# Bidirectional mLSTM encoder layer: the row work for a block of four chunks, done for both directions together and spread over the block before

## The chip, the cores and the metric

The kernel runs on one core of a Trainium2 chip. The metric is device time in microseconds (us) of one execution. TensorE (PE) does the matrix products, VectorE (DVE), ScalarE (ACT) and GpSimd (POOL) the elementwise work, and SyncE (SP) issues every transfer. Each engine goes through its own instructions in their written order, and they meet at semaphores.

## The reference

One hybrid layer on 2048 tokens of width 1024. Three mixers run on one normalised input (a bidirectional mLSTM, a neighbourhood attention, a cross-attention), are merged by gates, and an MLP follows. The change touches the mLSTM alone, four heads in each of two directions:

```
b = jnp.cumsum(lf, axis=-1)
d_log = jnp.where(tril, b[..., :, None] - b[..., None, :] + ig[..., None, :], -jnp.inf)
inter = b + m_st[..., None]
m_t = jnp.maximum(inter, jnp.max(d_log, axis=-1))
s = jnp.einsum('bhtd,bhsd->bhts', q, k) * jnp.exp(d_log - m_t[..., None])
w_inter = jnp.exp(inter - m_t)
num = einsum(s, v) + w_inter[..., None] * einsum(c_st, q)
den = jnp.sum(s, axis=-1) + w_inter * einsum(n_st, q)
h = num / jnp.maximum(jnp.abs(den), jnp.exp(-m_t))[..., None]
```

`lf` (log of the forget gate) and `ig` (input gate) are one number per head and token. From them come, per token, the running sum `b`, the running maximum `m`, and the rows `a = ig - b`, `r = b - m`, `w = exp(r + m of the chunk before)` and `exp(-m)`. This is the row work: the same few operations on 4 heads x 512 tokens.

## The kernel before

The layer has three phases. In phase 2, TensorE computes merge gates (`late_gates`, `gate`), a product of 24 matmuls of 128x512 per gate. After every sixth of them the code calls `tick()`, which advances the generator `ml_stream` by one step. So mLSTM instructions are put between gate matmuls. Gate results are taken out of PSUM by ACT (L599). There are two PSUM buffers for gates (`mm`) and two for most mLSTM tiles (`mx`).

`ml_stream` waits START_2 = 20 ticks, then goes through 32 slots of four ticks, forward and backward directions in turn, each with one chunk of 128 tokens (`ml_chunk`). Up to four chunks of a direction are in flight at different stages: the decay matrix (L809 on PE, L811 on ACT, L813 on POOL), scores (L827) and their product with the decay (`pt`, L829, which together with the copy L831 on ACT frees the scores' PSUM), a transposition of the keys (L838) with the scaled keys (`kw`, L844), outputs (L862, L865) and state (L871). On POOL the scaled query `qw` (L848) of a later chunk stands in the same queue; it reads the query tile `qk` (load L796) and the row weights `wb` (load L805).

Before the first chunk of a block of four chunks, `ml_block(d, b)` issues the whole row work of one direction: two loads, two scans on DVE (L749, L753), five further tensor operations on DVE, three copies or exponentials on ACT (L759, L762, L768), a store of `w`, and four small transpositions on PE (L772) of the running maximum `r_m`. The row tiles of both directions share one buffer of 36 partitions (direction 0 in rows 0 to 3, direction 1 in rows 32 to 35).

The order on PE is the order of the code. On the other engines a scheduler sets the order ahead of time, by when it believes inputs to be there and by how early the instruction stands in the code; at run time the order is fixed.

Of the kernel before, what the change touches and what calls it, by code (L numbers as in the profile page):

```python
# [12 lines left out]
F32 = mybir.dt.float32  # L13
F32R = mybir.dt.float32r
BF16 = mybir.dt.bfloat16
AF = mybir.ActivationFunctionType
ALU = mybir.AluOpType
# [6 lines left out]
TB = 512  # L24
# [56 lines left out]
class Body:  # L81
# [10 lines left out]
    def t(self, tag, shape, bufs, dt=F32):  # L92

        self.n += 1
        return self.p_a.tile(list(shape), dt, name=f"{tag}_{self.n}", tag=tag, bufs=bufs)
# [527 lines left out]
    def ml_stream(self):  # L623


        for _ in range(START_2):
            yield
        dirs = [list(range(16)), list(range(15, -1, -1))]
        live = [[], []]
        when = {0: [(2, 0)], 1: [(1, 1), (2, 1), (3, 0)], 2: [(1, 2)], 3: [(3, 0), (1, 3), (0, 1)]}  # L630
        d = 0
        while any(dirs) or any(live[0]) or any(live[1]):
            c = dirs[d].pop(0) if dirs[d] else None
            if c is not None and c % 4 == (0, 3)[d]:
                self.ml_block(d, c // 4)
            live[d] = [None if c is None else self.ml_chunk(d, c)] + live[d][:3]
            for tick in range(4):
                for age, _ in when[tick]:
                    if age < len(live[d]) and live[d][age]:
                        next(live[d][age], None)  # L640
                yield
            if len(live[d]) == 4:
                live[d][3] = None
            d = 1 - d
# [29 lines left out]
    def ml_consts(self):  # L674
        nc, p = self.nc, self.p_a
        t = lambda name, shape, dt=F32: p.tile(shape, dt, name=name)


        self.reset = t("reset", [36, TB])
        nc.vector.memset(self.reset, 1.0)  # L680
        nc.vector.memset(self.reset.rearrange("p (c t) -> p c t", t=128)[:, :, 0:1], 0.0)

        self.bd = t("bd", [36, 4, 128])
        nc.vector.memset(self.bd, 0.0)
        for d in range(2):
            nc.gpsimd.affine_select(out=self.bd, in_=self.bd, compare_op=ALU.not_equal, fill=1.0, base=-32 * d,
                                    pattern=[[-1, 4], [0, 128]], channel_multiplier=1)


        self.at, self.rd, self.rp = {}, {}, {}  # L690
        for d in range(2):
            for i in range(2):
                at = self.at[d, i] = t(f"at{d}{i}", [100, TB], F32R)
                rd = self.rd[d, i] = t(f"rd{d}{i}", [100, 4, 128], F32R)
                rp = self.rp[d, i] = t(f"rp{d}{i}", [36, TB])
                for x in (at, rd, rp):
                    nc.gpsimd.memset(x.bitcast(F32), 0.0)
                for k in range(2):
                    nc.vector.tensor_copy(rd[32 * k:32 * k + 4], self.bd[32 * k:32 * k + 4])
                    nc.vector.tensor_scalar(at[64 + 32 * k:68 + 32 * k], self.reset[32 * k:32 * k + 4], 0.0, 1.0, ALU.mult, ALU.add)  # L700
        self.carry = t("carry", [36, 1])
        nc.vector.memset(self.carry, NEG)
        self.packs = []
        self.rows = {}
        self.state = [None, None]
        self.gml = t("gml", [128, 512])
        raw = self.ev()
        nc.sync.dma_start(raw, self.a["g_mlstm"])
        nc.vector.tensor_scalar(self.gml, raw, 0.5, None, ALU.mult)
# [24 lines left out]
        nc.vector.scalar_tensor_tensor(l, f, 0.0, l, ALU.min, ALU.subtract)  # L734
        self.store(view(self.scr["lf"]), l)

    def ml_block(self, d, b):

        nc = self.nc
        n = b if d == 0 else 3 - b  # L740
        hs = slice(32 * d, 32 * d + 4)
        if d == 0:
            self.packs.append({x: self.row("r_" + x, (36, TB + (x == "m")), bufs=1) for x in "ifbmw"})
        P = {x: y[hs] for x, y in self.packs[n].items()}
        ig, lf, bs, m, w = (P[x] for x in "ifbmw")
        nc.sync.dma_start(ig, self.scr["ig"][4 * d:4 * d + 4, b * TB:(b + 1) * TB])
        nc.sync.dma_start(lf, self.scr["lf"][4 * d:4 * d + 4, b * TB:(b + 1) * TB])
        rev = (lambda x: x[:, ::-1]) if d else (lambda x: x)
        nc.vector.tensor_tensor_scan(rev(bs), self.reset[hs], rev(lf), 0.0, ALU.mult, ALU.add)  # L749
        cm, ce = (m[:, 1:], m[:, 0:1]) if d == 0 else (m[:, :TB], m[:, TB:])  # L750
        carry = self.carry[hs]
        nc.vector.tensor_copy(ce, carry)
        nc.vector.tensor_tensor_scan(rev(cm), rev(lf), rev(ig), ce, ALU.add, ALU.max)  # L753
        nc.vector.tensor_copy(carry, m[:, TB:] if d == 0 else m[:, 0:1])
        lo = slice(32 - 32 * d, 36 - 32 * d)
        at, rp = self.at[d, n % 2], self.rp[d, n % 2]
        a, r = ig, bs
        nc.vector.tensor_tensor(a, ig, bs, ALU.subtract)
        nc.scalar.activation(at[hs], a, AF.Copy)  # L759
        nc.vector.tensor_tensor(at[lo], a, at[hs].bitcast(F32), ALU.subtract)  # L760
        nc.vector.tensor_tensor(r, bs, cm, ALU.subtract)
        nc.scalar.activation(rp[hs].bitcast(F32R), r, AF.Copy)  # L762
        nc.vector.tensor_tensor(rp[lo], r, rp[hs], ALU.subtract)
        ms = (m[:, 0:TB] if d == 0 else m[:, 1:]).rearrange("p (c t) -> p c t", t=128)
        ms = ms[:, :, 0:1] if d == 0 else ms[:, :, 127:128]
        nc.vector.tensor_tensor(w.rearrange("p (c t) -> p c t", t=128), r.rearrange("p (c t) -> p c t", t=128),
                                ms.to_broadcast([4, 4, 128]), ALU.add)
        nc.scalar.activation(w, w, AF.Exp)  # L768
        self.store(self.scr["w"][d][b], w)
        p = self.ps("mx", (128, 4, 128))  # L770
        for c in range(4):
            nc.tensor.transpose(p[:, c, 0:4], cm[:, c * 128:(c + 1) * 128], self.ident[hs, hs])  # L772
        em = self.row(f"r_em{d}", (128, 4, 4))
        nc.scalar.activation(em, p[:, :, 0:4], AF.Exp, scale=-1.0)
        self.rows[d, b] = dict(at=at, rp=rp, em=em)

    def ml_chunk(self, d, c):

# [797 lines left out]
```

## Time and profile before

| | us |
|---|---|
| median of 3 runs | 2989.27 |
| lowest and highest | 2983.28, 2989.3 |
| the profiled execution | 2988.64 |
| its span, first to last instruction | 2986.9 |
| PE busy | 2910.6 (97%) |
| DVE busy | 2070.4 (69%) |
| ACT busy | 1195.1 (40%) |
| POOL busy | 237.1 (8%) |

PE is busy nearly throughout, so time is won or lost where PE waits. The clock granted to PE is listed by stretch as a share of 2.4 GHz: 1.00 or 0.50. Phase 2 lies at about 970 to 1345 us of the span.

### The profile page before, as it was taken

How to read it: one execution, taken by the hardware profiler on the slowest of the kernel's cores; microseconds unless marked ns; L12 is line 12 of the kernel's file. 1: busy time of each engine (PE TensorE's matmuls, PEld its weight loads, DVE VectorE, ACT ScalarE, POOL GpSimd, SP SyncE). 2: the span in 40 equal slices, each digit the busy share in tenths (PEclk: the TensorE clock that was granted, in tenths of full speed). 3: DMA queues.
4: the chain of work that ended last, by engine and by line, in shares of the span. 5: the costliest groups of instructions: out<-in, count | busy, mean ns of one | idle time of the engine just before them, and what ended most of it. 6: DMA issues, size and time to landing. Idle time of an engine off the chain costs nothing.

```text
span 2986.9 us, 41900 instructions
## 1 busy us (share of the span) xinstructions
PE 2910.6 (97%) x15028; PEld 2374.8 (80%) x15028; DVE 2070.4 (69%) x3557; ACT 1195.1 (40%) x2198; POOL 237.1 (8%) x389
## 2 busy tenths in 40 slices
PE   8999999999999899999999999999999999999999
PEld 6778788878877677778888888888878888888887
DVE  6676775567654765674769888666676888885666
ACT  6454654344543333342233333543312433344331
POOL 3020210011000322330000000000000000000000
PEclk9999999999999999999999999999999999999999
DMA  8776777867799667789535444766874444466655
GB/s 276 225 253 202 231 227 240 266 217 217 240 283 307 195 199 234 240 276 315 183 110 169 155 152 155 275 191 224 268 235 128 137 155 151 154 226 225 195 182 165
DMA packets 341712, 632.97 MB, mean 212 GB/s; under 512 B 29344, under 2 KB 151008, under 8 KB 341504
## 3 DMA queue, kind: packets, MB, share of 16 engines
q1 hardware_dynamic: 341504, 630.30, 65.4%
q8 instruction: 118, 1.93, 0.3%
q14 instruction: 90, 0.74, 0.1%
HBM read 453.63 MB, written 176.55 MB: 211 GB/s over the span
## 4 chain that ended last, share of the span: by engine, by line
PE 55%; DVE 2%; DMA 2%; issue 1%; ACT 0%; POOL 0%; SPq 0%; DVEq 0%; ACTq 0%; POOLq 0%
PE mm L232 18%; PE mm L234 18%; PE mm L233 18%; PE mm L1339 0%; DVE h L900 0%; DMA og<-s_o 0%; DMA wr<-in_w_units_dram 0%; DMA hf<-s_hf 0%; DVE ev L1495 0%; ACT hf L896 0%; POOL rs L325 0%; DVE acc L1488 0%; DVE ws L177 0%; DVE h L888 0%; DMA X<-s_a 0%
## 5 line engine op out<-in xcount | busy, mean ns | idle before, releaser
L232 PE MATMUL mm<-X,ws 128*128 128x512 f32 x1152 | 448.5, 389 | 0.0
L234 PE MATMUL mm<-X,ws 128*128 128x512 f32 x1152 | 448.2, 389 | 0.0
L233 PE MATMUL mm<-X,ws 128*128 128x512 f32 x1152 | 448.1, 389 | 0.0
L232 PE MATMUL mm<-hT,ws 128*128 128x512 f32 x896 | 375.6, 419 | 12.1 <-ACT cz L654 5.5
L177 DVE TENSOR_TENSOR ws<-wr,ws 128x1024 fp32r<-128x1024 f32 (+1 forms) x212 | 263.0, 1246 | 142.8 <-ACT ws L176 137.7
L234 PE MATMUL mm<-hT,ws 128*128 128x512 f32 x896 | 353.6, 395 | 0.0
L233 PE MATMUL mm<-hT,ws 128*128 128x512 f32 x896 | 353.4, 394 | 0.0
L233 PE MATMUL mm<-X 128*128 128x512 f32 x896 | 348.8, 389 | 2.5 <-DVE X L1462 2.5
L234 PE MATMUL mm<-X 128*128 128x512 f32 x896 | 348.7, 389 | 0.5 <-DVE X L1462 0.5
L232 PE MATMUL mm<-X 128*128 128x512 f32 x896 | 348.7, 389 | 0.4 <-ACT X L1461 0.4
L1461 ACT ACTIVATE X<-X 128x1024 fp32r<-128x1024 f32 x176 | 187.0, 1063 | 319.4 <-DMA X<-s_t 124.5
L1462 DVE TENSOR_TENSOR X<-X 128x1024 fp32r<-128x1024 f32 x176 | 214.3, 1224 | 132.8 <-ACT X L1461 132.0
L176 ACT ACTIVATE ws<-wr 128x1024 fp32r<-128x1024 f32 (+1 forms) x212 | 223.5, 1059 | 164.7 <-PE mm L234 91.8
L232 PE MATMUL mm<-ws,hT 128*128 128x512 f32 (+2 forms) x704 | 260.9, 371 | 9.3 <-ACT cz L654 5.1
L234 PEld LDWEIGHTS mm<-X,ws 128*128 128x128 f32 x1152 | 216.2, 188 | 45.1
L233 PEld LDWEIGHTS mm<-X,ws 128*128 128x128 f32 x1152 | 216.2, 188 | 44.9
L232 PEld LDWEIGHTS mm<-X,ws 128*128 128x128 f32 x1152 | 216.2, 188 | 44.5
L234 PE MATMUL mm<-ws,hT 128*128 128x512 f32 (+2 forms) x704 | 249.8, 355 | 1.1 <-DVE hT L434 1.1
L233 PE MATMUL mm<-ws,hT 128*128 128x512 f32 (+2 forms) x704 | 249.0, 354 | 0.3 <-DVE ws L177 0.3
L202 ACT ACTIVATE ws<-wr 128x512 fp32r<-128x512 f32 x224 | 135.3, 630 | 219.9 <-PE mm L234 139.3
L232 PEld LDWEIGHTS mm<-hT,ws 128*128 128x128 f32 x896 | 170.2, 190 | 54.1 <-issue 9.8
L234 PEld LDWEIGHTS mm<-hT,ws 128*128 128x128 f32 x896 | 169.6, 189 | 39.0
(266 smaller groups left out, 4855.3 us busy)
## 6 DMA issues: line engine op xcount, KB each, us to landing
wr<-in_w_units_dram SPq DMA_DIRECT2D x308, 512.0 KB
s_s<-u SPq DMA_DIRECT2D x32, 1024.0 KB
X<-s_s SPq DMA_DIRECT2D x64, 512.0 KB
X<-s_t SPq DMA_DIRECT2D x64, 512.0 KB
s_g<-ev SPq DMA_DIRECT2D x96, 256.0 KB
ev<-s_g SPq DMA_DIRECT2D x96, 256.0 KB
s_a<-u SPq DMA_DIRECT2D x96, 256.0 KB
X<-s_a SPq DMA_DIRECT2D x48, 512.0 KB
```

Of the source, the lines that this page charges most:

```text
L176: nc.scalar.activation(w[:, 0], raw, AF.Copy)
L177: nc.vector.tensor_tensor(w[:, 1], raw, w[:, 0].bitcast(F32), ALU.subtract)
L202: nc.scalar.activation(hi, src, AF.Copy)
L232: mm(out, lhs[0], rhs[0], start=first, stop=False)
L233: mm(out, lhs[0], rhs[1], start=False, stop=False)
L234: mm(out, lhs[1], rhs[0], start=False, stop=last)
L1461: nc.scalar.activation(hi, src, AF.Copy)
L1462: nc.vector.tensor_tensor(lo, src, hi.bitcast(F32), ALU.subtract)
```

## The change

`ml_block` is replaced by a generator `ml_rows(n)` that does the row work for block n of both directions in one go and yields between steps. `ml_stream` makes one step per tick. The rows of block 0 begin at tick 0 of the 20 ticks that were idle; those of block n + 1 begin at slot 8n + 3, five slots before they are needed. Four ticks pass between the loads and the first scan. `a`, `r` and the exponential of `w` are done once for all 36 partitions in place of once per direction. The five row tiles are allocated once and set to 0 by POOL (L711).

```diff
     def ml_stream(self):
+        rows = self.ml_rows(0)
         for _ in range(START_2):
+            next(rows, None)
             yield
+        slot = 0
...
             c = dirs[d].pop(0) if dirs[d] else None
-            if c is not None and c % 4 == (0, 3)[d]:
-                self.ml_block(d, c // 4)
+            if slot % 8 == 3 and slot < 24:
+                rows = self.ml_rows(slot // 8 + 1)
+            slot += 1
             live[d] = [None if c is None else self.ml_chunk(d, c)] + live[d][:3]
             for tick in range(4):
                 for age, _ in when[tick]:
                     if age < len(live[d]) and live[d][age]:
                         next(live[d][age], None)
+                next(rows, None)
                 yield
...
-        self.packs = []
+        self.pack = [t("r_" + x, [36, TB + 2 * (x == "m")]) for x in "ifbmw"]
+        for x in self.pack:
+            nc.gpsimd.memset(x, 0.0)
...
+    def ml_rows(self, n):
+        nc = self.nc
+        ig, lf, bs, m, w = self.pack
+        cm, a, r = m[:, 1:TB + 1], ig, bs
+        dirs = [(d, n if d == 0 else 3 - n, slice(32 * d, 32 * d + 4), slice(32 - 32 * d, 36 - 32 * d)) for d in range(2)]
+        rev = lambda d, x: x[:, ::-1] if d else x
+        for d, b, hs, _ in dirs:
+            for x, name in ((lf, "lf"), (ig, "ig")):
+                nc.sync.dma_start(x[hs], self.scr[name][4 * d:4 * d + 4, b * TB:(b + 1) * TB])
+        for _ in range(4):
+            yield
+        for d, _, hs, _ in dirs:
+            nc.vector.tensor_tensor_scan(rev(d, bs[hs]), self.reset[hs], rev(d, lf[hs]), 0.0, ALU.mult, ALU.add)
+            yield
+        for d, _, hs, _ in dirs:
+            ce = m[hs, 0:1] if d == 0 else m[hs, TB + 1:TB + 2]
+            carry = self.carry[hs]
+            nc.vector.tensor_copy(ce, carry)
+            nc.vector.tensor_tensor_scan(rev(d, cm[hs]), rev(d, lf[hs]), rev(d, ig[hs]), ce, ALU.add, ALU.max)
+            nc.vector.tensor_copy(carry, m[hs, TB:TB + 1] if d == 0 else m[hs, 1:2])
+            yield
+        nc.vector.tensor_tensor(a, ig, bs, ALU.subtract)
+        for d, _, hs, _ in dirs:
+            nc.scalar.activation(self.at[d, n % 2][hs], a[hs], AF.Copy)
+        nc.vector.tensor_tensor(r, bs, cm, ALU.subtract)
+        yield
+        for d, _, hs, lo in dirs:
+            at = self.at[d, n % 2]
+            nc.vector.tensor_tensor(at[lo], a[hs], at[hs].bitcast(F32), ALU.subtract)
+            nc.scalar.activation(self.rp[d, n % 2][hs].bitcast(F32R), r[hs], AF.Copy)
+        yield
+        for d, _, hs, lo in dirs:
+            rp = self.rp[d, n % 2]
+            nc.vector.tensor_tensor(rp[lo], r[hs], rp[hs], ALU.subtract)
+        yield
...
+        nc.scalar.activation(w, w, AF.Exp)
+        for d, b, hs, _ in dirs:
+            self.store(self.scr["w"][d][b], w[hs])
+        for d, b, hs, _ in dirs:
+            yield
+            p = self.ps("mx", (128, 4, 128))
+            for c in range(4):
+                nc.tensor.transpose(p[:, c, 0:4], cm[hs, c * 128:(c + 1) * 128], self.ident[hs, hs])
+            em = self.row(f"r_em{d}", (128, 4, 4))
+            nc.scalar.activation(em, p[:, :, 0:4], AF.Exp, scale=-1.0)
+            self.rows[d, b] = dict(at=self.at[d, n % 2], rp=self.rp[d, n % 2], em=em)
```

Three places show how this moves instructions. The first is PE at the first transpositions of phase 2. Before, those of the forward direction stand in the sixth gate (`mm_11001`), after its first six matmuls:

```order
L232 MATMUL mm_11001<-hT,ws_10832 128x512
L233 MATMUL mm_11001<-hT,ws_10832 128x512
L234 MATMUL mm_11001<-hT,ws_10832 128x512
L232 MATMUL mm_11001<-hT,ws_10832 128x512
L233 MATMUL mm_11001<-hT,ws_10832 128x512
L234 MATMUL mm_11001<-hT,ws_10832 128x512
L772 MATMUL mx_11028<-ident,r_m_11011 128x4 x4
```

Now they stand at the same place of the fourth gate (`mm_10972`), and those of the backward direction six matmuls behind them:

```order
L234 MATMUL mm_10972<-hT,ws_10619 128x512
L794 MATMUL mx_10979<-ident,r_m 128x4 x4
L232 MATMUL mm_10972<-hT,ws_10619 128x512
L233 MATMUL mm_10972<-hT,ws_10619 128x512
L234 MATMUL mm_10972<-hT,ws_10619 128x512
L232 MATMUL mm_10972<-hT,ws_10619 128x512
L233 MATMUL mm_10972<-hT,ws_10619 128x512
L234 MATMUL mm_10972<-hT,ws_10619 128x512
L794 MATMUL mx_10992<-ident,r_m 128x4 x4
```

Both have moved up by two gates, which is 48 matmuls for the forward direction.

The second place is DVE at the first two chunks, where `pt` and `kw` are the chunks' own work, `r_` and `at_` the row work of block 1, and `ws` a split of weights. Before:

```order
L829 TENSOR_TENSOR pt_1968_11154<-mx_11156,de_1967_11145 128x2x128
L749 SCALAR_TENSOR_TENSOR r_b_11647<-reset,r_f_11646 4x512
L844 TENSOR_TENSOR kw_1972_11176<-mx_11171,de_1967_11145 128x256
L753 SCALAR_TENSOR_TENSOR r_m_11648<-r_f_11646,r_m_11648,r_i_11645 4x512
L177 TENSOR_TENSOR ws_11126<-wr_11125,ws_11126 128x8x128
L754 COPY carry<-r_m_11648 4x1
L758 TENSOR_TENSOR r_i_11645<-r_i_11645,r_b_11647 4x512
L749 SCALAR_TENSOR_TENSOR r_b_11647<-reset,r_f_11646 4x512
L761 TENSOR_TENSOR r_b_11647<-r_b_11647,r_m_11648 4x512
L760 TENSOR_TENSOR at_10783<-r_i_11645,at_10783 4x512
L829 TENSOR_TENSOR pt_1982_11220<-mx_11221,de_1981_11211 128x2x128
```

Now:

```order
L851 TENSOR_TENSOR pt_1963_11156<-mx_11158,de_1962_11147 128x2x128
L866 TENSOR_TENSOR kw_1967_11178<-mx_11173,de_1962_11147 128x256
L177 TENSOR_TENSOR ws_11128<-wr_11127,ws_11128 128x8x128
L851 TENSOR_TENSOR pt_1977_11226<-mx_11227,de_1976_11217 128x2x128
L851 TENSOR_TENSOR pt_1977_11226<-mx_11228,de_1976_11217 128x2x128
L759 SCALAR_TENSOR_TENSOR r_b<-reset,r_f 4x512
```

The row work of block 1 is gone from between these chunks: it now stands ahead of the first `pt`, right behind that of block 0. The scan in the last row belongs to block 2.

The third place is SP ahead of the load of the third chunk's `qk`. Before, the row loads of block 1 stand directly in front of it:

```order
L746 DMA r_i_11645<-s_ig 4x512
L172 DMA wr_11257<-in_w_units_dram 128x1024
L747 DMA r_f_11646<-s_lf 4x512
L746 DMA r_i_11645<-s_ig 4x512
L747 DMA r_f_11646<-s_lf 4x512
L796 DMA qk_2010_11337<-s_qk 128x4x128
```

Now:

```order
L101 DMA s_w_137<-r_w 4x512
L101 DMA s_w_142<-r_w 4x512
L172 DMA wr_11263<-in_w_units_dram 128x1024
L827 DMA wb_2055_11573<-s_w_136 64x2x128 x2
L827 DMA wb_2077_11669<-s_w_143 64x2x128 x2
L818 DMA qk_2005_11348<-s_qk 128x4x128
```

The row loads have gone ahead, and two stores of `w` and four loads of `wb` stand between the weights and the `qk` load.

## Rows read from the trace of the kernel before

**Rows 1.** Waits of PE at 960 to 1360 us: us in total, times, longest

```profile
PE mx L838 <- ACT sk L831: 7.4, 3, 5.9
PE mm L232 <- DMA hT<-s_hT: 4.0, 1, 4.0
...
PE mm L232 <- ACT ev L599: 1.8, 1, 1.8
...
PE mx L827 <- ACT de L811: 2.2, 2, 1.1
PE mx L827 <- DVE C L877: 1.5, 3, 0.9
PE mx L827 <- DVE kw L844: 1.1, 1, 1.1
```

**Rows 2.** Windows: us, busy us and counts by engine, PEclk (granted clock), DMA share, GB/s

```profile
80.00:82.00 2.00, 1.93 (x12) 1.94 (x13) 1.97 (x5) 1.24 (x3) 0.00 (x0) 0.79 1.01 395
82.00:84.00 2.00, 2.00 (x5) 0.96 (x4) 1.97 (x3) 0.00 (x0) 0.00 (x0) 0.50 0.93 250
...
1008.00:1010.00 2.00, 2.00 (x11) 1.41 (x11) 1.67 (x2) 1.95 (x4) 1.43 (x2) 1.00 0.54 172
976.00:1344.00 368.00, 346.88 (x1954) 261.95 (x1953) 246.62 (x490) 141.69 (x380) 118.79 (x157) 0.99 0.72 228
...
974.00:976.00 2.00, 2.00 (x7) 1.52 (x7) 1.97 (x3) 0.43 (x2) 2.00 (x4) 0.64 1.03 385
...
1040.00:1042.00 2.00, 2.00 (x14) 1.28 (x12) 1.71 (x5) 1.01 (x2) 0.32 (x1) 0.92 0.78 244
```

**Rows 3.** Timeline of PE: start, us, what, [idle before <- releaser]

```profile
80.07 0.39 PE L232 MATMUL mm<-ws,hT 128*128 128x272 f32 x1 [2.37 <-ACT cz L654]
...
989.99 0.39 PE L232 MATMUL mm<-hT,ws 128*128 128x512 f32 x1
...
1001.19 0.41 PE L772 MATMUL mx<-ident,r_m 4*128 4x4 f32 x4
...
1007.75 0.50 PE L232 MATMUL mm<-hT,ws 128*128 128x512 f32 x1 [1.83 <-ACT ev L599]
```

**Rows 4.** Timeline of DVE at the first two scans of block 0

```profile
992.21 1.21 DVE L749 TENSOR_TENSOR_SCAN r_b<-reset,r_f 4x512 f32<-4x512 f32 x1 [3.29 <-DMA r_f<-s_lf]
993.35 1.25 DVE L753 TENSOR_TENSOR_SCAN r_m<-r_f,r_m,r_i 4x512 f32<-4x512 f32 x1
```

**Rows 5.** Timelines of SP, POOL, DVE and PE around the second chunk

```profile
1020.46 0.38 PE L838 MATMUL mx<-ident,qk 128*128 128x128 f32 x2
...
1021.77 0.55 SPq L796 DMA_DIRECT2D qk<-s_qk  x1
...
1027.04 2.08 POOL L848 TENSOR_TENSOR qw<-qk,wb 128x256 f32<-128x256 f32 x1 [7.67 <-PE mx L827]
1029.19 1.59 POOL L806 TENSOR_TENSOR rd<-bd,rp 36x512 fp32r<-36x512 f32 x1
1030.86 1.44 POOL L813 TENSOR_SCALAR_AFFINE_SELECT de<-de 128x512 f32<-128x512 f32 x1
...
1032.86 0.68 DVE L760 TENSOR_TENSOR at<-r_i,at 4x512 fp32r<-4x512 f32 x1
1033.57 0.76 DVE L829 TENSOR_TENSOR pt<-mx,de 128x256 f32<-128x256 f32 x2
...
1034.47 0.69 PE L838 MATMUL mx<-ident,qk 128*128 128x128 f32 x2 [5.89 <-ACT sk L831]
```

**Rows 6.** Three POOL lines in phase 2: count, ns min/median/max, first and last start

```profile
L806 POOL TENSOR_TENSOR rd<-bd,rp x32: 1262/1283/2275, 1000.6 to 1286.3; 36x512 fp32r<-36x512 f32 x32
...
L813 POOL TENSOR_SCALAR_AFFINE_SELECT de<-de x32: 631/637/1558, 1018.7 to 1325.9; 128x512 f32<-128x512 f32 x32
...
L848 POOL TENSOR_TENSOR qw<-qk,wb x30: 727/744/2082, 1012.2 to 1325.1; 128x256 f32<-128x256 f32 x30
```

**Rows 7.** Timeline of DVE in a slot without row work

```profile
1083.06 0.76 DVE L829 TENSOR_TENSOR pt<-mx,de 128x256 f32<-128x256 f32 x2 [1.69 <-PE mx L827]
```

More of the change, by code (lines that the diff above doesn't have):

```diff
@@ L735, in ml_logsig @@
         self.store(view(self.scr["lf"]), l)
-    def ml_block(self, d, b):
+    def ml_rows(self, n):
         nc = self.nc
[L740 to L757, printed above, removed]
@@ L758, in ml_block @@
+        for d, _, hs, _ in dirs:
[5 more added lines that the diff above has]
+            yield
         nc.vector.tensor_tensor(a, ig, bs, ALU.subtract)
-        nc.scalar.activation(at[hs], a, AF.Copy)
@@ L760, in ml_block @@
-        nc.vector.tensor_tensor(at[lo], a, at[hs].bitcast(F32), ALU.subtract)
+        for d, _, hs, _ in dirs:
+            nc.scalar.activation(self.at[d, n % 2][hs], a[hs], AF.Copy)
         nc.vector.tensor_tensor(r, bs, cm, ALU.subtract)
[L762 to L765, printed above, removed]
@@ L766, in ml_block @@
-        nc.vector.tensor_tensor(w.rearrange("p (c t) -> p c t", t=128), r.rearrange("p (c t) -> p c t", t=128),
-                                ms.to_broadcast([4, 4, 128]), ALU.add)
-        nc.scalar.activation(w, w, AF.Exp)
[L769 to L774, printed above, removed]
@@ L775, in ml_block @@
-        self.rows[d, b] = dict(at=at, rp=rp, em=em)
+        yield
[8 more added lines that the diff above has]
+        yield
+        for d, _, hs, _ in dirs:
+            ms = (m[hs, 0:TB] if d == 0 else m[hs, 2:TB + 2]).rearrange("p (c t) -> p c t", t=128)
+            ms = ms[:, :, 0:1] if d == 0 else ms[:, :, 127:128]
+            nc.vector.tensor_tensor(w[hs].rearrange("p (c t) -> p c t", t=128), r[hs].rearrange("p (c t) -> p c t", t=128),
+                                    ms.to_broadcast([4, 4, 128]), ALU.add)
```

## The prediction

> **What bounds the kernel now.** I read the page first (PE is busy nearly throughout), then the windows of phase 2, since only there the change moves anything. From 976 to 1344 us PE is busy 346.9 of 368 us, DVE 246.6, POOL 118.8 [rows 2]. So the order of gate matmuls on PE sets the end. Work on the other engines counts only where PE waits for it, and 121 idle us on DVE can hide it otherwise. Next I read PE's waits [rows 1] and placed each in the timeline. Those near row work are the wait of 1.8 us for a gate's copy (L599), 1.1 us for `kw`, 5.9 us at the second chunk's key transposition, and, at the beginnings of blocks 2 and 3, all of the 2.2 and 1.5 us at L827 and the 7.4 - 5.9 = 1.5 us that is left of L838: 5.2 us.
>
> A long wait costs twice, because the clock falls to 0.50 behind it. After the wait of 5.89 us PE goes on at 1034.47 [rows 5] with the clock low until about 1040.3 (at 1040 to 1042 it is 0.92, so low for 0.32 us): 5.8 us at half speed, 2.9 us lost. After the wait of 4.0 us, which ended at 968.9, the clock was low until 975.4 (0.64 in 974 to 976): 6.5 us, 3.2 lost. A wait of 2.37 us at 80.07 [rows 3] was followed by 0.79 and then 0.50 in two windows, at least 0.4 + 1.0 = 1.4 us lost. After the 1.83 us at 1007.75 the clock stayed at 1.00 [rows 2, 3]. So row work costs PE today 1.8 + 1.1 + 5.9 + 2.9 + 5.2 = 16.9 us in all: no more can be won.
>
> **The change part by part.**
>
> *A, the new wait at the first transpositions.* The 20 idle ticks looked free, but PE's order is that of the code. Step 12 of `ml_rows(0)` puts the forward transpositions 48 matmuls ahead of where they stood. Before, they began at 1001.19; sixteen groups of three matmuls back, PE is at 989.99 [rows 3]. Their input does not come earlier by as much: the first scan began at 992.21, when `r_f` landed (the load of a log that is itself computed at the beginning of phase 2), and the second scan, which makes `r_m`, ended at 993.35 + 1.25 = 994.6 [rows 4]. The new order on DVE keeps these two scans first, and the load is behind the same store. So PE waits 994.6 - 990.0 = 4.6 us where it did not wait before. For the clock I take 2.9 us, between the 2.9 and 3.2 of the two waits that are nearest in length, at their lower end because the backward transpositions, six matmuls on, give DVE's other two scans time (2.5 us; six matmuls at half speed take about 2.6). **A costs 7.5 us.** Bounds: 6.0 (clock at 1.4) and 9.8 (the loads land 2 us later, since SP now issues a `qk`, a `v` and a weights load ahead of them, and the clock costs 3.2).
>
> *B, the gate's copy.* L599 stood on ACT behind a copy of block 0's backward row, which waited for DVE; PE waited 1.83 us [rows 3]. Block 0's rows begin no later than before, and PE is 7.5 us later, so ACT has time. But block 1's four copies now stand ahead of the sixth gate's copy, so a similar wait can come back there. **B gains 1.8**, bounds 0 and 1.8.
>
> *C, the first two chunks.* Before, `kw` stood behind a scan that waited for a row load: 1.1 us. Then came the 5.9. Its chain [rows 5]: `qk` of the third chunk is issued at 1021.77; POOL's `qw`, which reads it, begins at 1027.04. The row names a matmul as releaser, but `qw` reads only what two loads bring, and stands in front of the second chunk's `rd` and decay mask on POOL. These three take 2.08 + 1.59 + 1.44 = 5.11 us beside DVE's row work, and 0.74 + 1.28 + 0.64 = 2.66 us by their medians [rows 6]. The mask ends at 1032.30, and DVE is then busy with row operations (the last is L760) until `pt` at 1033.57, 1.27 us later. PE goes on 0.90 us after that. With no row work between these chunks, `pt` comes 2.45 + 1.27 = 3.7 us earlier. The `qk` load can leave up to 0.9 us earlier: its tile is free after the first chunk's key transposition, which ended at 1020.46 + 0.38 = 1020.84, and SP has the 5.7 us by which PE is now late (A less B) to clear the loads ahead of it. PE would then go on at 1034.47 - 4.6 = 1029.9 and, without the `kw` wait, arrive 1.1 us before its old 1028.6, at 1027.5. A wait of 2.4 us stays, because the cause that is left is a load and not row work. It is as long as the one at 80.07, so the clock costs about 1.4 in place of 2.9. **C gains 4.6 + 1.5, about 6.** Bounds: 1.3 (only the 1.27 us of DVE go) and 9.9 (all of 1.1 + 5.9 + 2.9).
>
> The Trainium skill's page "SBUF — State Buffer", section "Who interferes with whom", says that a DVE instruction with two SBUF inputs and a GpSimd instruction that reads SBUF exclude each other: the second one blocks until the first is done. The `qw` of 2.08 us agrees (0.74 plus the scan's 1.25 is 1.99). If POOL's stretch were long for another reason, C would gain 2.45 less, and the sum would come to little over 1 us won.
>
> *D, blocks 2 and 3.* Their rows are spread, but since `r_m` is one buffer, the second scan of a direction must wait until PE has transposed that of the block before, five slots on. So a scan and two tensor operations stand together ahead of one `pt`: 1.25 + 0.68 + 0.68 = 2.6 us (the scan as in [rows 4], the others at the length of L760 [rows 5], whose tile has as many elements a row). In a slot without row work DVE is idle 1.69 us before `pt` [rows 7]. The rest, 0.9 us a block, I count as a wait of PE. **D gains 5.2 - 1.8 = 3.4**, bounds 0 and 5.2.
>
> *The rest is hidden.* Eight tensor operations (8 x 0.68 = 5.4 us of DVE) and four exponentials go; DVE's 121 idle us make that worth nothing. Five fills of the row tiles on POOL come while its next work waits for block 0's rows. The eight groups of transpositions are the same on PE, only elsewhere.
>
> Sum: 7.5 - 1.8 - 6 - 3.4 = -3.7 us. The profiled execution took 2988.6 (its span 2986.9 and 1.7 around it), 0.6 under the median of the three runs. Forecast: **2984.9 us**. What a measurement of this kernel can tell from no change is about 0.2%, or 6 us, so this is most likely no change that can be told.
>
> **The rivals.**
>
> 1. *The wait at the second chunk goes wholly.* If `qk` lands 2.4 us earlier, PE does not wait there and the clock stays up: C is 9.9, and the time is 2988.6 + 7.5 - 1.8 - 9.9 - 3.4 = 2981.0. For it: SP's load is late today because SP is busy. Against it: four `wb` loads and a weights load now stand right ahead of that load. 0.25.
> 2. *Slower: the wait at the second chunk stays.* If the `qk` load comes as late behind the stores of `w` for block 1 and the `wb` loads, and POOL is held as before, C is 1.3: 2988.6 + 7.5 - 1.8 - 1.3 - 3.4 = 2989.6, and 2991.9 with A at 9.8. It is slower from the point at which C gains less than 2.3. For it: the two stores of `w` on SP, ahead of the load, wait for the last operation of block 1's rows. 0.20.
> 3. *The new neighbour of POOL.* Block 1's rows now stand beside the four `rd` products of POOL, so DVE and POOL hold each other there; the rows end later, ACT's copies with them, and PE waits at the eighth gate for the sixth gate's copy. At the size of the old wait (1.83), B falls to 0: 2986.7. It is the skill's rule again, by which this place would not be free; no run here shows it. 0.07.
> 4. *The new wait does not arise*, because PE reaches the fourth gate late for another reason: 2988.6 - 1.8 - 6 - 3.4 = 2977.4. Nothing in the trace of before holds PE there. 0.05.
>
> The forecast itself has the remaining 0.43.
>
> **How the numbers follow.** The forecast's own range is 2983 to 2989 (A and D by about 2 either way). To the fast side the range reaches through rival 1, to 2978 (D at 5.2 as well); to the slow side through rival 2 with A at its upper bound, to 2993. Faster by over 0.2%: rival 4, most of rival 1 and the forecast's edge, 0.32. Slower by over 0.2%: rival 2 with A high and D at 0, 0.12. Within 0.2%: 0.56.
>
> **What would show it.** A: in the new trace PE has a wait of 4 to 5 us for `r_m` at L794 near 990 us, released by DVE's L765, with the clock at 0.50 behind it. B: no wait of PE for L599 near 1000 to 1025. C: the wait at the key transposition (now L860) between 1 and 3.5 us, POOL's three operations near 2.7 us together, and `kw` without a wait. D: PE's waits in blocks 2 and 3 of about 2 us in all. I am wrong if L794 does not wait, if the wait at the second chunk is over 4 us or nil, or if waits appear after 1200 us that were not there, where only transfers and the outputs are at work.

## The result

The changed kernel takes 2993.03 us (median of 20 runs, 2987.96 to 2998.81), the kernel before 2988.41 us in the same session (20 runs, 2980.35 to 2993.09). The ratio is 1.0021, 95% interval [1.0014, 1.0029]: about 4.6 us slower, where 3.7 us faster was forecast. The median lies just above the range. (The ratios here and below are those on record; they are not quotients of the two medians, which here give 1.0015, and differ from these by up to 0.001.)

### The profile page after: what moved, and what is told of

It reads as the page before. It is cut to its first block, busy times and chain, and to the rows that moved or that the text cites. A ratio compares the mean times of both kernels' runs of the same rounds, so it can differ in the third digit from the quotient of the medians.

```text
span 2986.3 us, 41896 instructions
## 1 busy us (share of the span) xinstructions
PE 2907.5 (97%) x15028; PEld 2374.9 (80%) x15028; DVE 2066.3 (69%) x3549; ACT 1193.7 (40%) x2194; POOL 237.9 (8%) x394
## 4 chain that ended last, share of the span: by engine, by line
PE 53%; DMA 2%; DVE 2%; issue 1%; ACT 1%; POOL 0%; SPq 0%; DVEq 0%; ACTq 0%; POOLq 0%
PE mm L232 18%; PE mm L234 17%; PE mm L233 17%; DMA wr<-in_w_units_dram 1%; PE mm L1361 0%; DMA hf<-s_hf 0%; DVE h L922 0%; DVE ws L177 0%; DVE ev L1517 0%; DVE acc L1510 0%; ACT hf L918 0%; POOL rs L325 0%; DMA og<-s_o 0%; DMA X<-s_s 0%; DMA X<-s_a 0%
## 5 line engine op out<-in xcount | busy, mean ns | idle before, releaser
L232 PE MATMUL mm<-X,ws 128*128 128x512 f32 x1152 | 448.5, 389 | 0.0
L234 PE MATMUL mm<-X,ws 128*128 128x512 f32 x1152 | 448.2, 389 | 0.0
L232 PE MATMUL mm<-hT,ws 128*128 128x512 f32 x896 | 376.6, 420 | 13.5 <-ACT cz L660 5.8
L234 PE MATMUL mm<-hT,ws 128*128 128x512 f32 x896 | 354.6, 396 | 0.0
L234 PE MATMUL mm<-X 128*128 128x512 f32 x896 | 348.7, 389 | 0.5 <-DVE X L1484 0.5
L232 PE MATMUL mm<-X 128*128 128x512 f32 x896 | 348.7, 389 | 0.0
L232 PE MATMUL mm<-ws,hT 128*128 128x512 f32 (+2 forms) x704 | 260.1, 369 | 7.6 <-ACT zif L528 5.2
L234 PEld LDWEIGHTS mm<-X,ws 128*128 128x128 f32 x1152 | 216.3, 188 | 45.0
L232 PEld LDWEIGHTS mm<-X,ws 128*128 128x128 f32 x1152 | 216.3, 188 | 44.6
L234 PE MATMUL mm<-ws,hT 128*128 128x512 f32 (+2 forms) x704 | 249.7, 355 | 1.6 <-DVE hT L434 1.6
L232 PEld LDWEIGHTS mm<-hT,ws 128*128 128x128 f32 x896 | 170.3, 190 | 55.0 <-issue 8.1
L234 PEld LDWEIGHTS mm<-hT,ws 128*128 128x128 f32 x896 | 170.3, 190 | 39.3
```

The source lines that it names most:

```text
L232: mm(out, lhs[0], rhs[0], start=first, stop=False)
L234: mm(out, lhs[1], rhs[0], start=False, stop=last)
```

## The profile after

The profiled execution took 2988.03 us with a span of 2986.3 us. First PE's waits at 960 to 1360 us, as in [rows 1]:

```profile
PE mx L794 <- issue: 6.7, 1, 6.7
PE mx L893 <- DVE hm L929: 6.2, 4, 2.6
PE mx L860 <- ACT sk L853: 4.3, 4, 1.8
PE mm L232 <- ACT ev L599: 4.2, 3, 2.1
PE mm L232 <- DMA hT<-s_hT: 2.8, 1, 2.8
PE mx L849 <- DVE C L899: 1.3, 1, 1.3
PE tr L926 <- DVE h L922: 1.1, 1, 1.1
```

The new wait at the transpositions (L794) is there. The 5.9 us at the second chunk's key transposition (L838, now L860) are gone: no wait there is over 1.8. But the gates' copies (L599) now cost 4.2 us in three waits, against 1.8 in one, and `hm` (L929) stands at 6.2 us. Where the first of these lie, in the timeline of PE:

```profile
980.83 0.50 PE L232 MATMUL mm<-hT,ws 128*128 128x512 f32 x1 [2.11 <-ACT ev L599]
...
994.68 0.55 PE L794 MATMUL mx<-ident,r_m 4*128 4x4 f32 x4 [6.74 <-issue]
...
1020.49 0.50 PE L232 MATMUL mm<-hT,ws 128*128 128x512 f32 x1 [1.62 <-ACT ev L599]
...
1037.94 0.44 PE L860 MATMUL mx<-ident,qk 128*128 128x128 f32 x2 [1.72 <-ACT sk L853]
```

Windows of the same kernel, with the columns of [rows 2]. The eighth and ninth column are the granted clock and the DMA share:

```profile
976.00:1344.00 368.00, 343.74 (x1946) 261.21 (x1945) 238.35 (x479) 139.66 (x383) 116.90 (x159) 0.98 0.73 228
988.00:990.00 2.00, 0.00 (x0) 0.00 (x0) 0.00 (x0) 0.21 (x1) 0.00 (x0) 1.00 0.92 306
990.00:992.00 2.00, 0.00 (x0) 0.00 (x0) 0.00 (x0) 0.00 (x0) 0.00 (x0) 0.63 0.91 336
992.00:1000.00 8.00, 5.32 (x18) 3.99 (x19) 7.64 (x9) 0.89 (x3) 0.00 (x0) 0.50 0.54 145
1000.00:1002.00 2.00, 2.00 (x9) 1.64 (x8) 1.90 (x4) 1.93 (x4) 0.00 (x0) 0.81 0.58 229
```

The clock falls during the wait and stays at 0.50 from the restart at 994.68 to 1000, then 0.81 on average for 2 us: some 6 us at half speed, 3 us lost.

To see where time goes I measured, in PE's timeline, from one gate matmul (L232 to L234) to another: from the first of phase 2 to the 241st (ten gates, in which the first three chunks start: the fill), from there to the 637th (the middle, up to block 3's transpositions, with which the row work ends), and to the 985th (the end). The second number of a pair is a second profile of the same kernel (runs before_again and after_again below).

| us | before | after | difference of the means |
|---|---|---|---|
| fill, ten gates | 77.1, 76.4 | 81.6, 83.4 | +5.7 |
| middle | 171.5, 171.4 | 167.8, 169.3 | -2.9 |
| end | 135.7, 133.1 | 136.9, 136.2 | +2.1 |

The sum, +4.9, is about the loss that the medians show. The fill repeats well: e10 and e6 below, whose one edit is used only behind it, add 77.4 to the kernel before and 81.7 to the changed one. The end does not: the two profiles of the kernel before differ by 2.6 us there, more than the +2.1. So the question is what makes the fill 5.7 us longer although its largest old wait is gone, and what happens at the end, where no row work is left.

## The experiments

The tables below give times after the first gate matmul of phase 2, since phase 2 begins up to 8 us earlier or later from one execution to the next (phase 1 is the same code in all kernels). I started from the theory that the new wait is the loss, and from rivals.

**e1**, the transpositions of block 0 later, and **e2**, only the forward ones early, in the kernel before:

```diff
 # e1, in ml_rows of the changed kernel
+        for _ in range(0 if n else 6):
+            yield
         for d, b, hs, _ in dirs:
             yield
             p = self.ps("mx", (128, 4, 128))
 # e2, in ml_stream of the kernel before
-        for _ in range(START_2):
+        for k in range(START_2):
+            if k == 12:
+                self.ml_block(0, 0)
             yield
```

> The changed kernel, with block 0's two groups of transpositions (L794) 36 matmuls further down PE's order (12 groups of three); DVE's, ACT's and the queues' work is as it was. Theory 1: the new wait of 6.7 us at these transpositions, with about 3 us of low clock behind it, is the cause of the loss. PE then reaches them at about 996.1, after r_m (994.6), so it does not wait, the clock stays at 1.00, and the time is 9 to 10 us under that of the changed kernel, 5 us under that of the kernel before (about 2983.5, ratio to before 0.9983). Rival 1: the time at the transpositions is slack that PE must wait out anyway, since the row products and the loads behind them end when they ended; then waits of 5 us and more appear at the first decay products (L831 in the changed kernel) or at the second chunk's key transposition, and less than 3 us come back (2990 or more). Rival 2: the loss comes from the new waits after 1200 us (hm, 6.2 us in four against 3.5): then the same.

> The kernel before, with nothing but block 0's forward row work (ml_block(0, 0)) issued eight ticks earlier, so that its transpositions stand where the changed kernel has them, 48 matmuls earlier in PE's order. Theory 1: PE gets there at about 988 to 990, r_m is ready at about 994.6 at the earliest, so it waits 5 to 7 us with the clock at 0.50 behind, and as nothing is gained elsewhere the time is 7 to 10 us over that of before (2996 to 2998, ratio 1.0025 to 1.0034). Rival 1: later waits (1.8 us for the sixth gate's copy, 5.9 us at the second chunk's key transposition) shrink by what PE is late, and the time is within 3 us of before.

e1: 2991.1 us, ratio to before 1.0017 [1.0008, 1.0026]. e2: 2986.8, ratio 0.9998 [0.9989, 1.0007]. Theory 1 falls by the times, from both sides. In e1 the wait at the transpositions is gone, and the fill takes 81.2 us, as in the changed kernel: the time is lost some 20 us further on, at the eighth gate (the expectations call it the seventh). Timelines of e1, ACT, DVE, POOL and PE:

```profile
1011.49 1.28 ACT L770 ACTIVATE at<-r_i 4x512 fp32r<-4x512 f32 x2 [9.52 <-DVE r_i L768]
1012.80 0.60 ACT L599 ACTIVATE ev<-mm 128x512 f32<-128x512 f32 x1
...
1001.90 4.46 DVE L759 TENSOR_TENSOR_SCAN r_b<-reset,r_f 4x512 f32<-4x512 f32 x2
...
997.50 7.78 POOL L830 TENSOR_TENSOR rd<-bd,rp 36x512 fp32r<-36x512 f32 x4 [23.45 <-DVE rp L780]
...
1013.45 0.79 PE L232 MATMUL mm<-hT,ws 128*128 128x512 f32 x1 [6.70 <-ACT ev L599]
```

A gate's copy stands on ACT behind two copies of block 1's rows, which wait 9.5 us for DVE; and DVE does block 1's scans at 1002, right behind the rest of block 0's row work, beside POOL's four `rd` products: two scans take 4.46 us there, where one takes 1.21 in [rows 4].

e2 has one thing against it. In its profile PE waits 5.6 us at the transpositions, as was meant, and the fill takes 80.0 us against 76.4 to 77.4. POOL then waits 5.2 us for PE's first decay product, and the first key transposition comes at 57.8 us after the first gate in place of 51.5. This execution was the slowest of e2's twelve (2991.5 us). The median shows no loss, and the interval leaves room for 0.07%, about 2 us: most of the wait with its low clock is slack, but not surely all.

**after_again** and **before_again** are the two kernels unchanged.

> The changed kernel once more, for a second profile. Theory 1: again 6 to 7 us of wait at L794 near 990, 1.5 to 2 us for the copies of gates 0 and 6, and no wait over 2 us at the second chunk. Rival 2: the waits for hm after 1200 us are again about 6 us in all; if they are 3.5 or less, they differ from one execution to the next and are no part of the change.

> The kernel before once more, for a second profile. Theory 1: the waits of phase 2 as in its first profile (4 us at the start for hT, 1.8 us for the sixth gate's copy, 5.9 us at the second chunk's key transposition), to within 1 us each. Rival 2: the waits for hm after 1200 us stay at 3.5 us.

They took 2993.44 and 2987.33 us. after_again waits 5.95 us at L794, 1.8 and 1.3 us for the two gate copies, but 3.0 us at the second chunk; for `hm` 6.0 us in four waits. before_again waits 2.9 us for hT, 1.6 for the sixth gate's copy, 5.89 at the second chunk, and for `hm` only 1.3. The differences that the theory names are those of the kernels, not of one execution.

**e3 and e4**: block 1's rows held back until the second chunk's `pt`, with and without the edit of e1. **e5**: e1 with block 1's copies on DVE. **e6**: `hm`'s first copy on DVE.

```diff
 # e3, e4: in ml_stream, ml_rows and ml_chunk
-            if slot % 8 == 3 and slot < 24:
+            if slot in (4, 11, 19):
...
+        if n == 1:
+            nc.vector.tensor_tensor(self.held, lf[:, 0:1], self.pt[0:36, 0, 0:1], ALU.add)
...
-        pt = self.t(f"pt{d}", [128, 4, 128], 1)
+        pt = self.pt = self.t(f"pt{d}", [128, 4, 128], 1)
 # e5: for n == 1, so for rp too
-            nc.scalar.activation(self.at[d, n % 2][hs], a[hs], AF.Copy)
+            nc.vector.tensor_copy(self.at[d, n % 2][hs], a[hs])
 # e6: in ml_chunk
-        nc.scalar.activation(hm[:, 0], p, AF.Copy)
+        nc.vector.tensor_copy(hm[:, 0], p)
```

> The kernel of e1 (late transpositions of block 0), in which block 1's row work is also held back: its loads, and with them its scans and copies, wait for one small DVE operation that reads the second chunk's pt (about 1033 in e1), and start one slot later in the code. Theory 2: PE's time between 1000 and 1035 us hangs on ACT, where the gates' copies (L599) stand behind copies of block 1's rows (6.7 us at the seventh gate in e1) and behind DVE's scans, lengthened beside POOL's rd products. Held back, these waits go (only the 1.4 us behind block 0's r_w stays), and PE reaches the second chunk 6 to 8 us earlier than in e1; the time is 5 to 8 us under e1, 2 to 4 under the kernel before (ratio 0.9986 to 0.9993). Rival 3: the fill's other chain (block 0's w, its store, the wb loads on SP, POOL's qw in front of rd and the decay mask) ends when it ended, so the two key transpositions (4.3 us in e1) wait as much longer, and less than 2 us are won against e1. Rival 4: the held rows now collide with chunks (DVE ahead of pt, as in the kernel before), with new waits of 3 us or more between 1040 and 1090.

> The changed kernel with block 1's row work held back as in e3, its transpositions of block 0 where the change put them. Theory 2: the wait at the transpositions stays at 6 to 7 us (plus the clock), the wait for the sixth gate's copy (1.3 to 1.6) goes, and DVE's work ahead of the first chunks gets shorter, so it gains 2 to 4 us on the changed kernel (2989 to 2991). Rival 3: no gain, as the wb loads hold the second chunk.

> The kernel of e1, with the four copies of block 1's rows (at and rp) done by DVE in place of ACT; its scans stay as early as in e1. If ACT's queue alone is the cause (theory 2), the 6.7 us at the seventh gate go to under 2, and the time is 4 to 6 us under e1, whether or not the fill follows; if the fill's other chain binds (rival 3), the wait at the gate goes too but comes back at the key transpositions, and less than 2 us are won.

> The changed kernel with the first copy of hm (L928) done by DVE in place of ACT, for all second-pass chunks. Theory 3: of the loss, 2 to 3 us come from after 1200 us, where ACT now has a weight conversion that waits for its load in front of the copy of hm, and PE waits for hm (6 us in all against 1.3 to 3.5 before). With the copy on DVE those waits fall to 2 us or less, and the time is 3 to 5 us under the changed kernel (2988 to 2990). Rival: DVE is late itself there, hm's waits stay over 4 us, and the time stays within 2 us.

| | us | ratio to before | fill, us | end, us |
|---|---|---|---|---|
| e3 | 2986.07 | 1.0006 [0.9996, 1.0015] | 77.5 | 138.3 |
| e4 | 2990.05 | 1.0013 [1.0004, 1.0022] | 78.0 | 137.3 |
| e5 | 2992.31 | 1.0023 [1.0014, 1.0033] | 82.7 | 136.8 |
| e6 | 2988.69 | 1.0001 [0.9990, 1.0011] | 81.7 | 133.9 |

Holding block 1's rows shortens the fill to 77.5 and 78.0 us, with the transpositions late or early (e4 still waits 4.2 us there). In the times less came of it: e3 missed the 0.9986 to 0.9993 that theory 2 asked, and the interval of e4 overlaps that of the changed kernel. e5 gains nothing, but it does not clear ACT: the exponential of block 1's `w` stayed there, and the first chunk's `de` stands behind it. Timelines of ACT and PE in e5:

```profile
1024.82 0.63 ACT L793 ACTIVATE r_w<-r_w 36x512 f32<-36x512 f32 x1 [11.50 <-DVE r_w L791]
1025.35 0.57 ACT L841 ACTIVATE de<-mx 128x512 f32<-128x512 f32 x1
...
1025.98 1.22 PE L857 MATMUL mx<-qk 64*128 64x128 f32 x6 [9.55 <-ACT de L841]
```

The wait moved from the gate's copy to the first chunk's scores. So the fill follows block 1's rows as a whole (e3, e4); which engine's queue hands the delay on, e5 does not tell. e6 shortens the end by 2.6 us (against the mean of the two profiles after). Theory 3 also asked that the waits for `hm` fall to 2 us or less, and they did not; only the long ones went (2.6 and 3.2 us in the two profiles after). PE's waits in e6:

```profile
PE mx L893 <- DVE hm L929: 5.1, 5, 1.6
```

**e7**: block 0's rows apart, forward first, by the old `ml_block`. **e8**: that, block 1 held, and the fills moved. **e9**: e8 with e6. **e10**: the kernel before with e6, as control.

```diff
 # e7, in ml_stream (ml_block is the old one, on the new tiles)
-        rows = self.ml_rows(0)
+        rows = iter(())
...
+            if slot < 2:
+                self.ml_block(slot, 3 * slot)
             slot += 1
 # e8 adds, beside the hold of e3 (in ml_consts and ml_rows)
-        for x in self.pack:
-            nc.gpsimd.memset(x, 0.0)
...
+            for x in (ig, bs, m[:, 1:TB + 1], w):
+                nc.vector.tensor_scalar(x, self.reset, self.pt[0:36, 0, 0:1], 0.0, ALU.mult, ALU.mult)
```

> The changed kernel with block 0's row work as in the kernel before: each direction alone and the forward one first, its transpositions at their old place; blocks 1 to 3 stay joint and early, and the fills of the row tiles stay on POOL. Theory 4: what the change lost at the beginning of phase 2 is a longer chain to the first chunk, since the forward rows now wait for the backward scans (w's exponential starts 40.9 us after the first gate matmul against 31.2, at's copy 33.8 against 27.3). Done apart, w's exponential starts at 33 or less (1.6 us late from POOL's fills), and the first key transposition at 54 to 58 us after the first gate in place of 63.5. Block 1's early rows still hold ACT and DVE, so the time is 2 to 4 us under the changed kernel. Theory 2 alone (block 1's rows are the whole cause): the first key transposition stays at 61 or later, and the time is within 1.5 us of the changed kernel.

> Both: block 0's row work apart and forward first as in the kernel before, block 1's held until the second chunk's pt as in e3, and the fills of the row tiles (four, since r_f needs none) moved from POOL's beginning to DVE behind that pt. Theories 2 and 4 together: gml is ready 13.4 us after the first gate as before, the first key transposition comes at 51 to 53 us (51.3 before), the second at 59 to 62 (65.2 before, since no row work stands between these chunks), the third 6 us earlier than before; blocks 1 to 3 keep their 2.5 us. So 5 to 8 us under the kernel before (ratio 0.9973 to 0.9984), with up to 3 us lost again to the waits for hm after 1200 us. Rival 3: the wb loads hold the second chunk, its key transposition stays at 64 to 66, and the gain is 1 to 3 us (0.9990 or more).

> The kernel of e8 with hm's first copy on DVE as in e6. Theory 3: the stretch after 1200 us is 2 to 3 us shorter than in the changed kernel, whatever order ACT was given, so 1 to 4 us under e8, and 6 to 10 under the kernel before (0.9967 to 0.9980).

> The kernel before with hm's first copy on DVE alone, the control for e6 and e9. If the waits for hm after 1200 us are the changed kernel's own (theory 3), it gains at most 1.5 us (0.9995 to 1.0005); if this copy is better on DVE anyway, it gains 3 us or more, and e6's gain says nothing on the change.

e7: 2989.8 us, 1.0006 [0.9998, 1.0015]. e8: 2987.8, 1.0008 [0.9999, 1.0018]. e9: 2982.18, 0.9986 [0.9977, 0.9995] (0.9967 to 0.9980 was asked). e10: 2985.64, 1.0001 [0.9992, 1.0010]. Milestones of the fill, in us after the first gate matmul, from one profile each (in the table, `w` and `wb` are of block 0):

| begins at | before | after | e4 | e7 | e8 | e11 |
|---|---|---|---|---|---|---|
| first scan (DVE) | 23.3 | 27.1 | 26.0 | 24.3 | 23.1 | 22.8 |
| exponential of the forward `w` (ACT) | 31.4 | 41.3 | 40.3 | 32.5 | 31.3 | 31.0 |
| exponential of the backward `w` (ACT) | 39.9 | 41.3 | 40.3 | 41.1 | 39.9 | 39.6 |
| issue of the first forward `wb` load (SP) | 35.5 | 51.9 | 45.7 | 36.5 | 35.3 | 35.0 |
| issue of the first backward `wb` load (SP) | 42.4 | 55.7 | 47.1 | 48.4 | 42.4 | 42.1 |
| second `qw`, backward (POOL) | 46.7 | 59.4 | 51.5 | 53.9 | 47.4 | 46.3 |
| first chunk's mask (POOL) | 49.8 | 62.5 | 56.0 | 57.0 | 51.0 | 49.3 |
| first key transposition (PE) | 51.5 | 64.0 | 58.0 | 60.7 | 57.2 | 51.2 |
| second key transposition (PE) | 65.5 | 72.8 | 66.4 | 70.1 | 65.7 | 61.1 |
| third key transposition (PE) | 76.9 | 81.4 | 77.8 | 80.3 | 76.2 | 72.6 |

This is the chain that sets the changed kernel's fill: the rows give `w`; `w` is stored and comes back as `wb`; `qw` reads `wb`, and two of them stand on POOL in front of the first chunk's mask, the second of them the backward direction's; the mask releases `pt`, and `pt` the scores' PSUM, which PE needs. Done jointly, the forward rows wait for the backward scans, and the exponential of the forward `w` starts 9.9 us later. That of the backward `w`, which the second `qw` needs, is only 1.4 us late. The other 11 us of the second `qw` are lost on the way to its load. Timelines of DVE, SP and POOL in the changed kernel (965.1 is the first gate):

```profile
1008.51 3.54 DVE L759 TENSOR_TENSOR_SCAN r_b<-reset,r_f 4x512 f32<-4x512 f32 x2
...
1012.41 2.58 DVE L765 TENSOR_TENSOR_SCAN r_m<-r_f,r_m,r_i 4x512 f32<-4x512 f32 x2
...
1015.37 1.23 DVE L177 TENSOR_TENSOR ws<-wr,ws 128x1024 fp32r<-128x1024 f32 x1
...
1009.14 7.81 SPq L172 DMA_DIRECT2D wr<-in_w_units_dram  x2
...
1020.84 2.53 SPq L827 DMA_DIRECT2D wb<-s_w  x4
...
1024.57 1.60 POOL L870 TENSOR_TENSOR qw<-qk,wb 128x256 f32<-128x256 f32 x1 [1.79 <-DMA wb<-s_w]
1026.25 1.29 POOL L828 TENSOR_TENSOR rd<-bd,rp 36x512 fp32r<-36x512 f32 x1
1027.61 0.64 POOL L835 TENSOR_SCALAR_AFFINE_SELECT de<-de 128x512 f32<-128x512 f32 x1
```

SP stands 7.0 us at a weights load, whose tile DVE frees with a split of weights (`ws`); the split stands behind block 1's scans, and all `wb` loads behind the weights load. Ahead of the backward ones SP waits 1.5 us more, to store the gate whose copy ends the wait at 1020.49. From the second `qw` on, POOL goes to the mask without a wait. A second path meets this one at `rd`, which also waits for PE's own first decay product: 0.7 us in the kernel before (nothing in before_again), 2.5 in e4, 1.6 in e8. Where it does, PE's order is the later of the two.

e7 brings the forward `w` back, and finds block 1's rows in the way further down: the backward `wb` leaves at 48.4 and the second `qw` starts at 53.9 against 46.7. The first key transposition comes at 60.7, where theory 4 asked 54 to 58, and the fill takes 80.4 us. e8 has both and still stands at 57.2 (and at 1.0008, where 0.9973 to 0.9984 was asked); its third place is in DVE's and POOL's timelines of e8:

```profile
1020.22 0.69 DVE L917 SCALAR_TENSOR_TENSOR og<-og,gml 128x512 f32<-128x512 f32 x1 [6.21 <-DMA og<-s_o]
1020.83 0.75 DVE L893 TENSOR_TENSOR pt<-mx,de 128x256 f32<-128x256 f32 x2
...
1015.58 0.64 POOL L877 TENSOR_SCALAR_AFFINE_SELECT de<-de 128x512 f32<-128x512 f32 x1
```

The mask is done at 1016.2, but `pt` stands behind a product for `og`, a tile that only the later half of the chunks uses, which waits 6.2 us for its load. The gap that the held rows left on DVE was given to it by the scheduler. Neither rival 3 nor my numbers had that.

**e11** (on e9) and **e12** (on e8) hold `og` back too.

```diff
+        if c == (5, 10)[d]:
+            og = self.t(f"og{d}", [128, 512], 1)
+            nc.vector.tensor_copy(og[:, 0:1], pt[:, 0, 0:1])
```

> The kernel of e9 with one more hold: the tile og, whose load and product belong to the second pass, gets a one-column copy of the sixth chunk's pt first, so that the scheduler can't put its product into DVE's queue ahead of the first chunk's pt. Theory 5: in e8 and e9 the first key transposition waits 4.0 and 5.3 us (57 us after the first gate against 51.3 before) only because pt stands behind og, whose load lands at 1020.2, while the decay mask is done at 1016.2. Held, it comes at 52 to 53, the second at 60 to 62, the third at 71 to 73 (76.7 in e9), and the time is 3.5 to 5 us under e9 and 7 to 9 under the kernel before (ratio 0.9970 to 0.9977). Rival 3: the second chunk stays at 65 to 66 because of the third chunk's qk load, which POOL's qw waits for; then less than 1.5 us are won.

> The kernel of e8 (hm's copy on ACT as in the changed kernel) with the same hold of og. Theory 5: the beginning of phase 2 as in e11; after 1200 us the waits for hm as ACT's order has them, so 3.5 to 5 us under e8 and 2 to 4 over e11 (ratio to before 0.9980 to 0.9992). Rival 3: within 1.5 us of e8.

e11: 2976.07 us against 2982.32 of before in the same session, 0.9972 [0.9961, 0.9983]. e12: 2980.88, 0.9992 [0.9983, 1.0001], 4.8 us over e11 where 2 to 4 was asked. The key transpositions came within 1 us of where theory 5 put them, and rival 3 falls; the fill takes 72.8 and 72.6 us. e11 is faster than both kernels. Its waits of PE at 960 to 1360 us:

```profile
PE mx L905 <- ACT sk L895: 5.0, 5, 2.9
PE mx L938 <- DVE hm L974: 4.8, 6, 1.6
PE mm L232 <- ACT ev L599: 2.8, 3, 1.6
PE mm L232 <- DMA hT<-s_hT: 2.6, 1, 2.6
PE mx L891 <- DVE C L944: 1.4, 1, 1.4
```

**The end.** Timelines of ACT and PE in the changed kernel, near 1250 us:

```profile
1247.04 0.60 ACT L599 ACTIVATE ev<-mm 128x512 f32<-128x512 f32 x1 [2.23 <-issue]
1250.79 1.06 ACT L176 ACTIVATE ws<-wr 128x1024 fp32r<-128x1024 f32 x1 [3.14 <-DMA wr<-in_w_units_dram]
1251.75 0.58 ACT L928 ACTIVATE hm<-tr 128x512 fp32r<-128x512 f32 x1
...
1255.16 0.66 PE L893 MATMUL mx<-v,kw 128*64 128x129 f32 x8 [2.60 <-DVE hm L929]
```

ACT's timeline at the same work in before_again:

```profile
1249.65 0.60 ACT L599 ACTIVATE ev<-mm 128x512 f32<-128x512 f32 x1 [1.06 <-PE mm L234]
1250.15 0.59 ACT L906 ACTIVATE hm<-tr 128x512 fp32r<-128x512 f32 x1
...
1253.12 1.06 ACT L176 ACTIVATE ws<-wr 128x1024 fp32r<-128x1024 f32 x1 [2.38 <-DMA wr<-in_w_units_dram]
```

The scheduler changed places of `hm`'s copy and a weight conversion, which waits 3.1 us for its load. With the copy on DVE the time falls by about 0.2% from e8 to e9 and from e12 to e11, each in one session, and not at all in the kernel before (e10). From the changed kernel to e6 the ratio falls as much, but by the medians e6 is still 3.2 us over the kernel before, against 4.6. In the profiles the end is shorter by 2.4 to 2.7 us of some 5 to 6; where the rest lies stays open. That the conversion's wait in front of the copy is what the edit removes is argued from these rows, since the waits for `hm` fell so little in e6.

## Why the prediction was wrong

**Sign and premise.** The step that failed is the first one: "the order of gate matmuls on PE sets the end", so that waits of PE can be added up one by one. That holds in the middle. In the fill it does not: the chain in the table above runs beside PE, and a wait that is removed on PE is met again where this chain ends. That is why the 10 us at the transpositions did not come back when removed (e1), and cost at most about 2 us when put in alone (e2, with the reservation made there). With it failed the step "The rest is hidden": row work that was moved ahead of the first chunk had no price in the sum, and the second `qw`, which stands in front of that chunk's mask, starts 12.7 us later.

**A** was right in place and kind, and too small: 6.7 us of wait and 3 of clock, for 4.6 and 2.9. Part of it is that phase 2 began 3.8 us earlier in this execution and PE arrived at 987.9. But counted from the first gate the scan's load was also 3.8 us late (27.1 against 23.3), and my upper bound had 2. Then its cost was booked as a loss of its own, which e1 refutes, and e2 by its times.

**The fills were not hidden.** "Five fills of the row tiles on POOL come while its next work waits" is true of POOL, but they slow down DVE beside them. DVE's timeline at the last copies of the constants, in before_again:

```profile
979.83 0.41 DVE L699 CAST rd<-bd 4x512 fp32r<-4x512 f32 x1
```

The same copy in after_again, with POOL's timeline beside it:

```profile
978.20 0.73 DVE L705 CAST rd<-bd 4x512 fp32r<-4x512 f32 x1
...
977.86 0.80 POOL L711 MEMSET r_w<- 36x512 f32 x1
```

`gml` is ready 15.0 us after the first gate in place of 13.4, and so is all that follows on DVE; the first gate's copy, which stands behind it, costs the wait at 980.83. With the fills moved (e8) it is 13.4 again.

**B** had the wrong sign. The old wait went, one of 1.6 us came at the eighth gate, and block 1's four copies stand in front of the gate's copy on ACT: this is rival 3, which I gave 0.07. Its size there is small because PE comes late; in e1, where PE comes earlier, it is 6.7 us.

**C** came near its place and was still the wrong count. From the first to the second key transposition it took 14.0 us before and takes 8.8 now, 5.2 us less where about 6 was forecast (10.1 in after_again, 3.7 less than in before_again). POOL's three operations, at 1034.21 to 1037.01, take 2.65 us together, as forecast; that the scan alone held them before was read wrongly, since it ended 0.4 us after `qw` had begun and a split of weights ran beside most of it. But the row work did not vanish from there: it moved ahead of the first chunk, whose key transposition went from 51.5 to 64.0 us. I followed what left the place and not where it went, though the order on DVE showed it "right behind that of block 0", and I did not see that doing both directions together puts the forward rows, the ones needed first, behind the backward scans, nor that SP's loads would stand behind it: "SP has the 5.7 us by which PE is now late" to clear them, I wrote, and SP spent 7.0 us waiting for DVE.

**D** was right: 3.4 forecast, 2.9 measured over the middle, where PE's waits fell from 5.2 to 2.5 us.

**After 1200 us** I named new waits as what would make me wrong, and gave them no price. They cost 2.1 us in the profiles. Rival 2 ended on the right side, but not by its cause, which was a wait at the second chunk that stays: 1.7 us were left of 5.9 (3.0 in after_again).

Together: fill +5.7 (forecast 7.5 - 1.8 - 6 = -0.3), middle -2.9 (-3.4), end +2.1 (0). In the profiles the fill carries most of the error. The times leave the shares open: e6 repairs only the end, with a fill of 81.7 us, and its ratio is 1.0001, while e12 repairs only the fill and has 0.9992. That block 1's early rows hold the chain is shown by e3 and e4; that the joint rows of block 0 with the fills on POOL do, by e3 against e11 and e12 (77.5 us against 72.8 and 72.6; in none of these does the first `pt` wait behind `og`); that `og` does in their absence, by e8 against e12. The joint rows and the fills were not parted, and how much each costs alone can't be said, since they hide one another.

## What to carry to other kernels

Where a pipeline fills, look for the chain from the first load to the first steady step and follow what moves onto it: the waits of the busy engine there are largely one slack seen at several places, and removing one shows the next. Follow it through the queue that issues the loads, too: one load that waits for its buffer holds all behind it (7.0 us here). Work that is joined is as late as its latest input, so what is needed first is better done apart. And where a scheduler orders the engines ahead of time, an idle stretch that an edit makes is given to whatever seems ready, with a late load in front of urgent work; a real dependency keeps it out (e3, e11).

## What was not expected of the hardware

A copy on DVE of 0.41 us took 0.73 beside POOL's fills, and a fill 0.80 in place of the 0.52 us that POOL's fills take where DVE does none of these copies. The Trainium skill's page "SBUF — State Buffer", section "Who interferes with whom", says that copies and casts on DVE can enter a mode in which they and GpSimd block each other for a whole instruction; these rows agree in that both operations take longer; whether one waits for the whole of the other they don't show. I had cited the section only for operations with two inputs. Two scans beside POOL's products took 4.46 us, and the four products 7.78, which is 1.9 us each against the 1.28 of [rows 6]. And the clock's price is not that of the wait's length alone: in e4, with a wait of 4.2 us at the transpositions, it was still at 1.00 when PE went on at 994.94, and then 0.94, 0.50 and 0.70 in the three windows of 2 us from 994: worked out 3.4 us at half speed, 1.7 us lost, where I took 2.9 for 4.6 us.
